# VectorE takes an output weight's low half first in a step; the opening norms two tiles at a time and evicts ahead of the last pair

## The chip, the cores and the metric

The kernel runs on one core of one Trainium2 chip. The metric is device time in microseconds (us) of one execution; several runs are given, and the figure is their median.

## The reference

One layer of a diffusion backbone is applied to 128 context tokens and to 2048 latent tokens, with the same weights but two modulations (`c_ctx` and `c`). Width 1024, everything in float32:

```
mod  = silu(c) @ w_mod + b_mod                      # shift, scale, gate, twice
h    = rmsnorm(x, norm1) * (1 + scale1) + shift1
z    = h @ w_in                                     # conv parts, q, k, v, o, gates
y_sc = short gated convolution of three 512-wide parts
h_m  = bidirectional mLSTM of q, k, v, gates; normed per head, times sigmoid(o)
x    = x + gate1 * (concat(y_sc, h_m) @ w_out)
h2   = rmsnorm(x, norm2) * (1 + scale2) + shift2
x    = x + gate2 * (silu(gg) * a @ w_down)          # a, gg: convolved halves of h2 @ w_up
y    = rmsnorm(x, final_norm)
```

Outputs are y for both token groups and the final mLSTM states of the context.

## The kernel before

All 2176 tokens are one sequence, held transposed: channels on the 128 partitions, tokens along the row. `BL` cuts it into six blocks: 0 to 4 of 384 tokens, 5 of 256. Block 0 holds the context tokens, so it has two spans with different modulation (`spans`). A 1024-wide activation is eight tiles, k = 0 to 7, of 128 channels.

Each float32 product is done as three matmuls of a narrower type: every operand is split in a high half (a rounded copy, made by ScalarE) and a low half (the rest, by a subtraction on VectorE or GpSimd), and `gemm` (L217) adds high x high, low x high and high x low for each k. So a tile is no use to TensorE until its low half is written: `hH`/`hL` for activations, `wh`/`wl` for weights.

**The opening** (L673 to L733). Its instructions keep the order in which they are written, engine by engine (`in_order(0)`, L733); those that are written later may be put between them by the planner, which orders each engine by its own estimate of when an operand is ready and by the order of writing. The modulation is computed on TensorE (`mods`), two column tiles at a time; in between come the norms. `apply` (L187) norms a block's tiles. For each k, VectorE multiplies (L196); for an even k ScalarE writes the high half (L200) and VectorE the low half (L201); for an odd k ScalarE adds the shift (L204), then copies the high half (L205), and GpSimd writes the low half (L206). `norm(b, rb, *ks)` (L696) calls it for the tiles that it names. Block 3 is normed in small pieces between the `mods`, block 4 at the end, four pairs of tiles.

`vg_first(k)` (L658) is block 3's value and gate product for one k: six accumulators, three chunks of 128 tokens by two column halves, each with three matmuls of 264 columns. Four of these are the four banks that `acc_tile` hands out in turn (`pa`, `pa1`); two are the halves of `y`, a two-bank tile. `vg_out` (L393) evicts one: GpSimd sets the ones column of a `row`, ScalarE copies (L396), SP's queue stores, and VectorE adds the gate bias from the same bank (L398). Then, at the end of the opening, `squares(5, ...)` (L172) sums the squares of block 5: ScalarE squares, VectorE adds (L184).

After that `vg((4,), hs, ws)` makes block 4's six value/gate tiles, with `prep(5, ss)` (L758) as a second generator that goes on by one step behind each tile. Its first step is empty, in its second `inv_rms` (L141) takes block 5's sum over the partitions on TensorE (L147) and its power on VectorE and GpSimd, in its third `apply` norms block 5. `vg((5,), ...)` and the heads (L426) follow, with side work in between: `mod_dve` computes the other 32 modulation tiles with products on VectorE, two per tile, into `y`; `first_stats` sums squares of blocks 0 to 2.

**The output projection.** From the mLSTM's last stage to the start of the feed-forward part each engine keeps the written order (`in_order(first)`, L1210). `out_proj` (L562) has 48 steps: one block and one 128-wide column tile of `w_out` each, one `gemm`. The head of a step on VectorE was written so (L597 to L610):

```
hook()                      # Feed: low halves of y for coming steps (L560)
load_r(k + 2)
while squared: add(...)     # token sums of squares (L589)
if len(behind) > 1: ...     # store, ScalarE's square
while trail: trail.pop()()  # wl of a weight split in the step before (L130)
```

`trail` has an entry only for the weights that `split_w` splits after step 20; GpSimd makes the low halves of the others. Then come the matmuls and VectorE's residual addition (L619), which frees the accumulator. From about step 22 on, `sums` (L249) puts work of the next stage behind each step: VectorE's product L272 and sums L283 to L291.

Of the kernel before, what the change touches and what calls it, by code (L numbers as in the profile page):

```python
# [10 lines left out]
F32 = mybir.dt.float32  # L11
F32R = mybir.dt.float32r
AF = mybir.ActivationFunctionType
# [7 lines left out]
KT = 8  # L21
# [30 lines left out]
def spans(t0, t1):  # L52

    return [(a, b, v) for a, b, v in ((t0, min(t1, P), 0), (max(t0, P), t1, 1)) if a < b]
# [3 lines left out]
def hymba_kernel(ctx: ExitStack, tc: tile.TileContext, I, O):  # L58
# [125 lines left out]
            V.tensor_add(ss[:, :n], ss[:, :n], sq[:, :n])  # L184
        return ss

    def apply(b, xt, norm, ks=range(KT), rb=None, pair=None):  # L187
        t0, n = BL[b]
        rb = spread(rcol(b), n) if rb is None else rb
        hH, hL = pair or h_pair()  # L190
        sh = 0 if norm == 0 else 24
        for k in ks:
            x = xt[k // 4][:, k % 4]
            for a, e, v in spans(t0, t0 + n):
                a, e = a - t0, e - t0
                V.scalar_tensor_tensor(x[:, a:e], x[:, a:e], ab[:, norm, k, v:v + 1], rb[:, a:e],  # L196
                                       op0=ALU.mult, op1=ALU.mult)
                sv = modT[:, sh + k, v:v + 1]
                if k % 2 == 0:
                    S.activation(hH[:, k, a:e], x[:, a:e], AF.Identity, bias=sv)  # L200
                    V.scalar_tensor_tensor(hL[:, k, a:e], x[:, a:e], sv, hH[:, k, a:e].bitcast(F32),  # L201
                                           op0=ALU.add, op1=ALU.subtract)
                else:
                    S.activation(x[:, a:e], x[:, a:e], AF.Identity, bias=sv)  # L204
                    S.activation(hH[:, k, a:e], x[:, a:e], AF.Copy)  # L205
                    G.tensor_sub(hL[:, k, a:e], x[:, a:e], hH[:, k, a:e].bitcast(F32))  # L206
        return hH, hL

    def h_pair():
# [158 lines left out]
    with ExitStack() as ph1:  # L368
# [193 lines left out]
        def out_proj(grps, defer, ws, hook):  # L562


            steps = [(g, m, b) for g, grp in enumerate(grps) for mp in range(0, KT, 2) for b in grp for m in (mp, mp + 1)]

            def load_r(k):
                if k < len(steps):
                    _, m, b = steps[k]
                    t0, n = BL[b]  # L570
                    xr = rp.tile([P, 384], F32, name="row")
                    Q.dma_start(xr[:, :n], I["x"][m][:, t0:t0 + n])
                    rows.append(xr)

            def close(b, m, xr):
                t0, n = BL[b]
                Q.dma_start(xD[m][:, t0:t0 + n], xr[:, :n])
                if m == 0:
                    second = b in grps[1]
                    sq = sss[b] = (rq if second else ssp).tile([P, 384], F32, name="cr" if second else "ss")  # L580
                else:
                    sq = sqp.tile([P, 384], F32, name="sq")
                S.activation(sq[:, :n], xr[:, :n], AF.Square)
                return b, m, sq

            def add(b, m, sq):
                n = BL[b][1]
                if m:
                    V.tensor_add(sss[b][:, :n], sss[b][:, :n], sq[:, :n])  # L589

            rows, got, trail, behind, squared, held, sss = [], [], [], [], [], [], {}
            for k in range(2):
                load_r(k)
            yield
            for k, (g, m, b) in enumerate(steps):
                grp, (t0, n) = grps[g], BL[b]
                hook()  # L597
                load_r(k + 2)
                while squared:
                    add(*squared.pop())  # L600
                if len(behind) > 1:
                    squared.append(close(*behind.pop(0)))
                while trail:
                    trail.pop()()
                if k - k % 4 + 4 < len(steps):
                    if k % 4 < (2 if k < 24 else 1):
                        got.extend(get_w(I["w_out"][steps[k + 4 + i][1]]) for i in range(1 if k < 24 else 2))
                    elif k % 4 > 1:
                        ws.append(split_w(got.pop(0), trail=trail if k > 20 else None))
                w, xr = ws[m % 2], rows.pop(0)  # L610
                acc = gemm(w, early[b], n)
                if k % 4 == 3:
                    del ws[:2]
                if held and k == held[0] + 4:
                    stats(held[1], [sss[b] for b in held[1]])
                    held = []
                for a, e, v in spans(t0, t0 + n):
                    a, e = a - t0, e - t0
                    V.scalar_tensor_tensor(xr[:, a:e], acc[:, a:e], modT[:, 16 + m, v:v + 1], xr[:, a:e],  # L619
                                           op0=ALU.mult, op1=ALU.add)  # L620
                behind.append((b, m, xr))
                if k % 16 == 15:
                    held = [k, grp]
                if k == len(steps) - 1:
                    for x in squared + [close(*x) for x in behind]:
                        add(*x)
                    defer.append(lambda: stats(grp, [sss[b] for b in grp]))
                hook(True)
                yield
# [3 lines left out]
        with tc.tile_pool(name="start", bufs=1, side="right") as stp:  # L633
# [24 lines left out]
            def vg_first(k):  # L658

                if k == 0:  # L660
                    y = pm.tile([P, 2, 512], F32, name="y")
                    vacc.extend([acc_tile() for _ in range(4)] + [y[:, 0], y[:, 1]])
                hH, hL = hs[3]
                for i in range(6):
                    j, c = divmod(i, 3)
                    w_h, w_l = (x[:, (k % 4) * 264:(k % 4 + 1) * 264] for x in ws[2 * j + k // 4])
                    a_h, a_l = hH[:, k, c * P:(c + 1) * P], hL[:, k, c * P:(c + 1) * P]
                    PE.matmul(vacc[i][:, :264], a_h, w_h, start=(k == 0), stop=False)
                    PE.matmul(vacc[i][:, :264], a_h, w_l, start=False, stop=False)
                    PE.matmul(vacc[i][:, :264], a_l, w_h, start=False, stop=(k == KT - 1))  # L670
# [23 lines left out]
            S.activation(rb, spread(rcol(3), 384)[:, :384], AF.Copy)  # L694

            def norm(b, rb, *ks):  # L696
                apply(b, xs[b], 0, ks, rb, hs[b])

            norm(3, rb, 0, 1)
            raw = get_vg(1)  # L700
# [24 lines left out]
            vg_first(5)  # L725
            norm(4, rb4, 4, 5)
            vg_first(6)
            norm(4, rb4, 6, 7)
            vg_first(7)
            ss = squares(5, xs[5])  # L730
            for i in range(6):
                vg_out(BL[3][0] // P + i % 3, i // 3, vacc[i])
            in_order(0)  # L733
            cB = stp.tile([P, 2, 1024], F32, name="cB")

# [20 lines left out]
                    yield  # L756

            def prep(b, ss):  # L758
                yield
                inv_rms(ss, BL[b][1], rcol(b))  # L760
                yield
                hs[b] = apply(b, xs[b], 0)
                yield
# [801 lines left out]
```

## Time and profile before

| | |
|---|---|
| median of 3 runs | 2499.62 us (2497.85 to 2501.0) |
| profiled execution | 2501.65 us |
| its span, first to last instruction | 2499.9 us |
| mean granted TensorE clock | 0.993 of full speed |
| busy: PE / weight loads / DVE / ACT / POOL | 98% / 94% / 66% / 45% / 21% |
| DMA | 447.61 MB, mean 179 GB/s |

PE is TensorE, PEld its weight loads, DVE is VectorE, ACT ScalarE, POOL GpSimd, SP SyncE with its DMA queue. Busy time is the time in which an engine has an instruction under way. An arrow `<-` names what ended an idle time, by the last semaphore event. The granted clock is TensorE's clock as a share of 2.4 GHz.

### The profile page before, as it was taken

To read this page: it belongs to the slowest core of one execution; us is meant where nothing else is said; L and a number is where in the kernel's file an instruction comes from. 1 tells how busy PE (TensorE), PEld (TensorE's weight loads), DVE (VectorE), ACT (ScalarE), POOL (GpSimd) and SP (SyncE) were. 2 spreads that over 40 slices of the span, in tenths; PEclk is the share of its full clock that TensorE was granted. 3 is DMA by queue.
4 is the path that set the end of the run, shared out by engine and by line. 5 is a ranking of instruction groups with operands and counts; after the bars stand their busy time and mean duration, and the time that the engine had idled before them with its cause. 6 is when DMAs were issued, how large, how long until landed. Compare 5 with 4: busy or idle time off the path is not lost. (4 is left out here: it accounts for less than half of the span.)

```text
span 2499.9 us, 42503 instructions
## 1 busy us (share of the span) xinstructions
PE 2450.5 (98%) x16127; PEld 2349.4 (94%) x16127; DVE 1638.6 (66%) x2682; ACT 1126.6 (45%) x2075; POOL 520.6 (21%) x468
## 2 busy tenths in 40 slices
PE   8899999999999999999999999999999999999998
PEld 8899999999999999989999999878888899999998
DVE  4893452332355675687668667877777786787586
ACT  3521243324445564465445445555555553444342
POOL 2433223211334351012112111122112200000000
PEclk9899999999999999999999999999999999999999
DMA  8673783265767886755126212622222286866674
GB/s 304 224 263 120 247 273 121 95 200 174 227 209 227 279 279 230 270 192 184 70 76 210 83 68 92 219 94 100 84 86 93 86 257 201 261 203 215 185 231 129
DMA packets 283102, 447.61 MB, mean 179 GB/s; under 512 B 23298, under 2 KB 208274, under 8 KB 280978
## 3 DMA queue, kind: packets, MB, share of 16 engines
q1 hardware_dynamic: 282898, 444.90, 54.1%
q8 instruction: 127, 2.08, 0.3%
q14 instruction: 77, 0.63, 0.1%
HBM read 336.82 MB, written 107.98 MB: 178 GB/s over the span
## 5 line engine op out<-in xcount | busy, mean ns | idle before, releaser
L224 PE MATMUL acc<-hH,wh 128*128 128x384 f32 (+1 forms) x1536 | 510.3, 332 | 1.0 <-ACT row L421 0.9
L226 PE MATMUL acc<-hH,wl 128*128 128x384 f32 (+1 forms) x1536 | 504.6, 329 | 2.9 <-DVE wl L130 2.6
L225 PE MATMUL acc<-hL,wh 128*128 128x384 f32 (+1 forms) x1536 | 503.1, 328 | 0.0
L1456 PE MATMUL d<-bh,wh 128*128 128x272 f32 x1232 | 356.4, 290 | 0.7 <-ACT raw L1314 0.7
L1458 PE MATMUL d<-bh,wl 128*128 128x272 f32 x1232 | 356.8, 290 | 0.0
L1457 PE MATMUL d<-bl,wh 128*128 128x272 f32 x1232 | 356.1, 289 | 0.0
L1302 PE MATMUL pa<-tH,wh 128*128 128x288 f32 (+1 forms) x1056 | 347.2, 329 | 3.2 <-DVE raw L1316 1.3
L1304 PE MATMUL pa<-tH,wl 128*128 128x288 f32 (+1 forms) x1056 | 345.9, 328 | 1.4 <-POOL wl L347 0.8
L1303 PE MATMUL pa<-tL,wh 128*128 128x288 f32 (+1 forms) x1056 | 346.5, 328 | 0.5 <-DVE tL L329 0.4
L347 POOL TENSOR_TENSOR wl<-st,wh 128x512 fp32r<-128x512 f32 x123 | 171.3, 1393 | 693.4 <-ACT wh L346 689.4
L226 PEld LDWEIGHTS acc<-hH,wl 128*128 128x128 f32 x1536 | 289.4, 188 | 5.7 <-DVE wl L130 5.4
L224 PEld LDWEIGHTS acc<-hH,wh 128*128 128x128 f32 x1536 | 289.7, 189 | 1.7 <-ACT row L421 1.3
L225 PEld LDWEIGHTS acc<-hL,wh 128*128 128x128 f32 x1536 | 289.7, 189 | 0.3 <-issue 0.2
L133 POOL TENSOR_TENSOR wl<-wst,wh 128x512 fp32r<-128x512 f32 (+1 forms) x136 | 198.7, 1484 | 424.4 <-ACT wh L127 371.1
L1245 DVE SCALAR_TENSOR_TENSOR tt<-raw,fw,tt 128x127 f32<-128x127 f32 (+4 forms) x264 | 245.6, 950 | 3.4 <-ACT tt L1251 2.3
L1456 PEld LDWEIGHTS d<-bh,wh 128*128 128x128 f32 x1232 | 232.6, 189 | 1.3 <-ACT raw L1314 1.1
L1457 PEld LDWEIGHTS d<-bl,wh 128*128 128x128 f32 x1232 | 232.6, 189 | 0.2
L1458 PEld LDWEIGHTS d<-bh,wl 128*128 128x128 f32 x1232 | 232.5, 189 | 0.0
L1302 PEld LDWEIGHTS pa<-tH,wh 128*128 128x128 f32 x1056 | 198.0, 188 | 19.7 <-ACT raw L1314 1.3
L1304 PEld LDWEIGHTS pa<-tH,wl 128*128 128x128 f32 x1056 | 198.6, 188 | 17.5 <-POOL wl L347 1.1
L1303 PEld LDWEIGHTS pa<-tL,wh 128*128 128x128 f32 x1056 | 198.2, 188 | 16.6 <-DVE tL L329 1.0
L346 ACT ACTIVATE wh<-s 128x512 fp32r<-128x512 f32 x176 | 110.7, 629 | 168.8 <-PE pc L1303 88.2
(268 smaller groups left out, 4830.9 us busy)
## 6 DMA issues: line engine op xcount, KB each, us to landing
st<-in_w_up SPq DMA_DIRECT2D x88, 512.0 KB, 4.6
us<-uD SPq DMA_DIRECT2D x48, 544.0 KB, 5.0
wst<-in_w_in SPq DMA_DIRECT2D x48, 512.0 KB, 3.9
uD<-tt SPq DMA_DIRECT2D x44, 544.0 KB, 2.7
R<-nD SPq DMA_DIRECT2D x34, 512.0 KB, 4.1
wm<-in_w_modr SPq DMA_DIRECT2D x32, 512.0 KB, 5.8
wst<-in_w_out SPq DMA_DIRECT2D x24, 512.0 KB, 3.7
st<-wsD SPq DMA_DIRECT2D x32, 384.0 KB, 3.9
```

The source lines that it names most:

```text
L133: G.tensor_sub(wl[:, a:a + n // 2], st[:, a:a + n // 2], wh[:, a:a + n // 2].bitcast(F32))
L224: PE.matmul(acc[:, :n], w_h, hH[:, k, :n], start=(k == 0), stop=False)
L225: PE.matmul(acc[:, :n], w_h, hL[:, k, :n], start=False, stop=False)
L226: PE.matmul(acc[:, :n], w_l, hH[:, k, :n], start=False, stop=(k == KT - 1))
L347: (G if on_pool else V).tensor_sub(wl, a, wh.bitcast(F32))
L1245: V.scalar_tensor_tensor(o, i, w, o, op0=ALU.mult, op1=ALU.add)
L1302: PE.matmul(acc, wh[:, w], rh, start=(kk == 0 and i in (0, 1, 5)), stop=False, skip_group_check=True)
L1303: PE.matmul(acc, wh[:, w], rl, start=False, stop=False, skip_group_check=True)
L1304: PE.matmul(acc, wl[:, w], rh, start=False, stop=(kk == 3), skip_group_check=True)
L1456: PE.matmul(acc, wh[:, c], uh, start=(kk == 0), stop=False)
L1457: PE.matmul(acc, wh[:, c], ul, start=False, stop=False)
L1458: PE.matmul(acc, wl[:, c], uh, start=False, stop=(kk == KH - 1))
```

## The change

Three edits. In `out_proj` the low half `wl` is taken at the head of a step, ahead of the feed and the token sums. `apply` takes groups of tiles: within a group first all products, then all ScalarE passes, then all low halves; `norm` passes its tiles as one group, every other caller keeps groups of one. In the opening `vg_first(7)` and three evictions stand ahead of the norm of block 4's last two tiles, the other three evictions behind it, and all ahead of block 5's squares; `prep` gets a second empty step.

```diff
-    def apply(b, xt, norm, ks=range(KT), rb=None, pair=None):
+    def apply(b, xt, norm, groups=[(k,) for k in range(KT)], rb=None, pair=None):
         t0, n = BL[b]
         rb = spread(rcol(b), n) if rb is None else rb
         hH, hL = pair or h_pair()
         sh = 0 if norm == 0 else 24
-        for k in ks:
-            x = xt[k // 4][:, k % 4]
-            for a, e, v in spans(t0, t0 + n):
-                a, e = a - t0, e - t0
-                V.scalar_tensor_tensor(x[:, a:e], x[:, a:e], ab[:, norm, k, v:v + 1], rb[:, a:e],
-                                       op0=ALU.mult, op1=ALU.mult)
-                sv = modT[:, sh + k, v:v + 1]
+        parts = [(a - t0, e - t0, v) for a, e, v in spans(t0, t0 + n)]
+        for ks in groups:
+            each = [(k, xt[k // 4][:, k % 4, a:e], hH[:, k, a:e], hL[:, k, a:e], modT[:, sh + k, v:v + 1], a, e, v)
+                    for k in ks for a, e, v in parts]
+            for k, x, h, l, sv, a, e, v in each:
+                V.scalar_tensor_tensor(x, x, ab[:, norm, k, v:v + 1], rb[:, a:e], op0=ALU.mult, op1=ALU.mult)
+            for k, x, h, l, sv, *_ in each:
                 if k % 2 == 0:
-                    S.activation(hH[:, k, a:e], x[:, a:e], AF.Identity, bias=sv)
-                    V.scalar_tensor_tensor(hL[:, k, a:e], x[:, a:e], sv, hH[:, k, a:e].bitcast(F32),
-                                           op0=ALU.add, op1=ALU.subtract)
+                    S.activation(h, x, AF.Identity, bias=sv)
                 else:
-                    S.activation(x[:, a:e], x[:, a:e], AF.Identity, bias=sv)
-                    S.activation(hH[:, k, a:e], x[:, a:e], AF.Copy)
-                    G.tensor_sub(hL[:, k, a:e], x[:, a:e], hH[:, k, a:e].bitcast(F32))
+                    S.activation(x, x, AF.Identity, bias=sv)
+                    S.activation(h, x, AF.Copy)
+            for k, x, h, l, sv, *_ in each:
+                if k % 2 == 0:
+                    V.scalar_tensor_tensor(l, x, sv, h.bitcast(F32), op0=ALU.add, op1=ALU.subtract)
+                else:
+                    G.tensor_sub(l, x, h.bitcast(F32))
         return hH, hL
...
             for k, (g, m, b) in enumerate(steps):
                 grp, (t0, n) = grps[g], BL[b]
+                while trail:
+                    trail.pop()()
                 hook()
                 load_r(k + 2)
                 while squared:
                     add(*squared.pop())
                 if len(behind) > 1:
                     squared.append(close(*behind.pop(0)))
-                while trail:
-                    trail.pop()()
...
             def norm(b, rb, *ks):
-                apply(b, xs[b], 0, ks, rb, hs[b])
+                apply(b, xs[b], 0, [ks], rb, hs[b])
...
             norm(4, rb4, 4, 5)
             vg_first(6)
+            vg_first(7)
+            for i in range(3):
+                vg_out(BL[3][0] // P + i, 0, vacc[i])
             norm(4, rb4, 6, 7)
-            vg_first(7)
+            for i in range(3):
+                vg_out(BL[3][0] // P + i, 1, vacc[3 + i])
             ss = squares(5, xs[5])
-            for i in range(6):
-                vg_out(BL[3][0] // P + i % 3, i // 3, vacc[i])
             in_order(0)
...
             def prep(b, ss):
+                yield
                 yield
                 inv_rms(ss, BL[b][1], rcol(b))
                 yield
```

## Rows read from the trace of the kernel before

**Rows 1.** The page: busy us, share of the span, instructions.
```profile
PE 2450.5 (98%) x16127; PEld 2349.4 (94%) x16127; DVE 1638.6 (66%) x2682; ACT 1126.6 (45%) x2075; POOL 520.6 (21%) x468
```

**Rows 2.** Stretches: length, PE, PEld, DVE, ACT, POOL busy, clock, DMA, GB/s.
```profile
62.00:75.00 13.00, 0.58 (x4) 0.43 (x3) 7.70 (x16) 8.98 (x22) 3.18 (x9) 0.63 0.51 206
...
82.00:100.00 18.00, 18.00 (x150) 18.00 (x150) 17.92 (x41) 11.63 (x29) 3.70 (x8) 1.00 0.69 223
```

**Rows 3.** TensorE's timeline, end of the opening: start, duration, line, idle before.
```profile
61.90 0.28 PE L670 MATMUL y<-wh,hL 128*128 128x264 f32 x1
74.61 0.99 PE L147 MATMUL st<-ones,ss 128*128 128x1 f32 x4 [12.42 <-DVE gates L398]
75.45 0.57 PE L411 MATMUL acc<-wh,hH 128*128 128x264 f32 x1
```

**Rows 4.** VectorE's timeline, norm of block 4 and squares of block 5.
```profile
64.04 0.95 DVE L201 SCALAR_TENSOR_TENSOR hL<-xs,modT,hH 128x384 fp32r<-128x384 f32 x1 [1.22 <-ACT hH L200]
64.91 1.12 DVE L196 SCALAR_TENSOR_TENSOR xs<-xs,ab,st 128x384 f32<-128x384 f32 x2
67.25 0.95 DVE L201 SCALAR_TENSOR_TENSOR hL<-xs,modT,hH 128x384 fp32r<-128x384 f32 x1 [1.22 <-ACT hH L200]
...
70.57 3.88 DVE L184 TENSOR_TENSOR ss<-ss,sq 128x256 f32<-128x256 f32 x7 [1.85 <-ACT sq L183]
```

**Rows 5.** ScalarE's timeline of the same stretch.
```profile
54.07 1.90 ACT L742 ACTIVATE cB<-cB 128x2048 f32<-128x2048 f32 x1
...
63.41 0.60 ACT L200 ACTIVATE hH<-xs,modT 128x384 fp32r<-128x384 f32 x1
65.55 0.61 ACT L204 ACTIVATE xs<-xs,modT 128x384 f32<-128x384 f32 x1 [1.54 <-DVE xs L196]
66.19 0.52 ACT L205 ACTIVATE hH<-xs 128x384 fp32r<-128x384 f32 x1
...
73.76 1.19 ACT L396 ACTIVATE row<-acc 128x256 f32<-128x256 f32 x4
```

**Rows 6.** Stretches of 2 us: length, PE busy, clock, DMA share, GB/s.
```profile
62.00:64.00 2.00, 0.18 (x2) 1.00 1.03 416
...
70.00:72.00 2.00, 0.00 (x0) 0.50 0.01 4
...
78.00:80.00 2.00, 2.00 (x16) 0.77 0.73 139
```

**Rows 7.** ScalarE's timeline: evictions of block 4's first, third and sixth tile.
```profile
80.25 0.39 ACT L396 ACTIVATE row<-acc 128x256 f32<-128x256 f32 x1 [0.65 <-PE acc L413]
...
86.28 0.37 ACT L396 ACTIVATE row<-acc 128x256 f32<-128x256 f32 x1
...
95.29 0.39 ACT L396 ACTIVATE row<-acc 128x256 f32<-128x256 f32 x1
```

**Rows 8.** TensorE's waits, 130 to 2500 us: total, times, longest.
```profile
PE acc L226 <- DVE wl L130: 2.6, 5, 0.7
```

**Rows 9.** GpSimd's timeline: low half of an odd tile of block 4.
```profile
63.58 1.00 POOL L206 TENSOR_TENSOR hL<-xs,hH 128x384 fp32r<-128x384 f32 x1 [2.22 <-ACT hH L205]
```

**Rows 10.** GpSimd's timeline: the last low half of block 5.
```profile
93.29 1.04 POOL L206 TENSOR_TENSOR hL<-xs,hH 128x256 fp32r<-128x256 f32 x1
```

**Rows 11.** VectorE's timeline: the head of a step of `out_proj`.
```profile
985.91 1.02 DVE L560 TENSOR_TENSOR hL<-xt,hH 128x384 fp32r<-128x384 f32 x2
986.85 0.55 DVE L589 TENSOR_TENSOR cr<-cr,sq 128x384 f32<-128x384 f32 x1
987.32 1.21 DVE L130 TENSOR_TENSOR wl<-wst,wh 128x1024 fp32r<-128x1024 f32 x1
```

**Rows 12.** TensorE's timeline: the matmul that waits for that `wl`.
```profile
988.59 0.44 PE L226 MATMUL acc<-hH,wl 128*128 128x384 f32 x1 [0.66 <-DVE wl L130]
```

**Rows 13.** ScalarE's timeline: the high half of the same weight.
```profile
981.86 1.06 ACT L127 ACTIVATE wh<-wst 128x1024 fp32r<-128x1024 f32 x1 [0.64 <-DMA wst<-in_w_out]
```

**Rows 14.** VectorE's timeline: a product of `mod_dve`.
```profile
77.34 1.23 DVE L751 SCALAR_TENSOR_TENSOR y<-wm,cB 128x1024 f32<-128x1024 f32 x1
```

## The prediction

> **What bounds the kernel now.** I read the busy times first: TensorE is busy 98% of the span [rows 1], so only what removes TensorE's idle time or raises its clock can move the end. The table by stretches says where the missing time is: in 62 to 75 us TensorE worked 0.58 us of 13.00, at a mean granted clock of 0.63; from 82 us it is full, and so is VectorE [rows 2]. TensorE's timeline gives the hole its edges: the last matmul of `vg_first(7)` starts at 61.90, and the next thing in its queue is `inv_rms` of block 5 at 74.61, after 12.42 us, put down to VectorE's gate additions [rows 3]. So behind the first value/gate tile lies a serial tail on VectorE and ScalarE: the norm of block 4, pair of tiles after pair, then block 5's squares and their adds, and only then the evictions of the six accumulators from 73.76 on [rows 4, 5]. The clock is 1.00 (2.4 GHz) in 62 to 64 us, 0.50 (1.2 GHz) by 70 us, and 0.77 on the mean in 78 to 80 us, when TensorE has worked again since 74.6 [rows 6]. So block 4's first tile, begun at 75.45 [rows 3], is evicted at 80.25, 4.8 us later, where three later tiles took 95.29 - 86.28 = 9.0 us, 3.0 each [rows 7]. The hole therefore costs 12.4 + (4.8 - 3.0) = 14.2 us.
>
> The table of waits has a smaller one late in the kernel: TensorE waits 2.6 us, in five pieces of at most 0.7, for the `wl` that VectorE writes in `out_proj` [rows 8].
>
> **The change part by part.**
>
> *Normed tiles two at a time.* Before, a pair of block 4 takes 67.25 - 64.04 = 3.21 us between two low-half subtractions [rows 4]. That is one chain: the subtraction of the even tile, VectorE's product of the odd tile, ScalarE's two passes of the odd tile, ScalarE's pass of the next even tile. In the new order both products come first, then ScalarE's three passes, then the subtractions. The chain is a product at 0.56 (half of 1.12), ScalarE's 0.60 and a subtraction at 0.95: 2.1 us [rows 4, 5]; ScalarE by itself needs 0.60 + 0.61 + 0.52 = 1.73, less [rows 5]. I take 2.0 per pair: the 0.95 holds a wait beside GpSimd's own subtraction of 1.00 us [rows 9], which in the new order lies mostly beside the products.
>
> On that point the Trainium skill, "SBUF — State Buffer", section "SBUF: two separate sides", is harsher than my 2.0: GpSimd and a VectorE operation with two SBUF inputs shut each other out for a whole instruction. The 0.95 us row fits it, as this subtraction began in the middle of GpSimd's. At its worst alignment the rule would hold the subtraction up for a whole GpSimd operation, a pair would take 2.8 us, and over the three pairs ahead of the first evictions the gain would be some 2 us smaller.
>
> *Evictions ahead of the last pair and of the squares.* At about 53.5 us ScalarE begins block 3's last two tiles (1.73), and there the planner has put the 1.90 us silu of `cB` [rows 5]; so it comes to block 4 at about 57.1. Three pairs at 2.0 end on it at 63.1; an eviction is 0.30 (1.19 for four [rows 5]) and VectorE's gate addition some 0.1 more, so the first bank is free at 63.5. TensorE idles 1.5 us instead of 12.4, and 62 to 64 us still shows clock 1.00 [rows 6]. The price: the additions wait for the evictions, and behind them in VectorE's queue stand the products of tiles 6 and 7, which start at 64.1. A product (0.56), ScalarE (1.73) and GpSimd (1.00) later, at 67.4, tile 7's low half is ready. Block 4's first value/gate tile comes to k = 7 at 63.5 + 7/8 x 3.0 = 66.1: another stall of 1.3 us. `inv_rms` of block 5, now between tiles, is still to be paid: 0.84 us at half clock (75.45 - 74.61 [rows 3]), about 0.5 at full. Sum: 14.2 - 1.5 - 1.3 - 0.5 = 10.9. I take 11.5, since the planner may fill the second stall with the next tile's first matmuls or put the silu elsewhere (up to 1.9). Bounds: with pairs as slow as before, 3.21, the three end 3.6 us later and the last adds 1.2, which leaves 6.1; with neither stall left it is 13.7.
>
> *One more empty step in `prep`.* It puts `inv_rms` and the norm of block 5 one tile of block 4 later, behind the third and the fourth. Block 5's squares with their seven adds (3.88 us [rows 4]) follow the last evictions, from about 67.3, so its sum is there by 72, before the third tile ends at 63.5 + 1.3 + 9.0 = 73.8. From the third tile's eviction to GpSimd's last low half it took 93.29 + 1.04 - 86.28 = 8.05 us before [rows 7, 10]. The fourth tile now ends at 77.3 (with the 0.5), so block 5 is ready at 85.4; TensorE comes to its first tile at 83.3 and to the last k at 85.9. No stall, but the margin falls from 95.29 + 2.6 - 94.33 = 3.6 us to 0.5.
>
> *VectorE takes `wl` first.* Only the weights split after step 20 go this way, twelve in all. From 985.91 on VectorE does two feed subtractions (1.02), a token add (0.47 to the next start), and then `wl`, from 987.32 to 988.53 [rows 11]; TensorE, which had waited 0.66 us, goes on at 988.59 [rows 12]. With `wl` at 985.91 it ends at 987.12, before TensorE's wait began at 987.93. A step without feed subtractions gains the 0.47 of the add alone. The rest keeps its place: the residual addition that frees the accumulator still comes behind all of these, no later; the feed subtractions come 1.21 us later, but for a step at least one ahead; the token sums have no reader until their group ends. What `wl` itself waits for, ScalarE's high half, is done at 981.86 + 1.06 = 982.92 [rows 13]. I take 2.3 of the 2.6; bounds 0 (VectorE has no idle time there, so that the next of its results may be late in place of each) and 2.6.
>
> *`apply` elsewhere* (blocks 0, 1, 2 and 5) has groups of one tile, and only block 0 with its two spans is reordered. I take 0, between -0.6 and 0.6 by one product.
>
> Sum: 11.5 + 2.3 = 13.8 us off the profiled execution's 2501.65: 2487.9. The median of the runs is 2.0 below that execution; against it 2485.8. I forecast 2486.
>
> **The rivals.**
>
> *A. The transfers don't come forward with TensorE* (12%). The DMA queues are full in 62 to 64 us (1.03) and idle in 70 to 72 (0.01) [rows 6]. If the heads' weights are limited by transfer, only that hole of about 6 us can be won back: 6 + 2.3 = 8.3 us, 2491. For it: the side work loads in the same stretch. Against: TensorE is full from 82 us on [rows 2], without a wait for a load.
>
> *B. The opening's hole stays* (8%), because `inv_rms` of block 5 is still put first on TensorE. Then the squares, now behind the evictions, hold TensorE until about 72 us with the clock down: 2 to 3 us won there, some 5 in all, 2495. For it: just that order stands in the old trace [rows 3]. Against: there the first tile could not have started either, as its bank's eviction began at 73.76; now the bank is free some 9 us ahead of the sum.
>
> *C. The other side: filler work on VectorE gets ahead of block 5* (5%). The `mod_dve` products (1.23 us each [rows 14]) need the accumulator pair that is now freed by 67.5, just when block 5's adds and norm come up, and VectorE is full later (17.92 of 18 us [rows 2]). Each product ahead of block 5's norm costs 1.23 us once the 0.5 us margin is gone. It decides from (13.8 + 0.5)/1.23 = 12 products on; with 16 the kernel loses 19.7 - 0.5 - 13.8 = 5.4 us: 2505.
>
> *D. The `wl` part gives nothing* (within the forecast's own range): 2488.
>
> **How the numbers follow.** The forecast with D, 2481 to 2490, has 70%; A 12%, B 8%, C 5%; 5% for stalls that come or go in the planned part behind the opening, either way. About 0.2% (5 us) is what can be told from no change, so faster is below 2494.6 and slower above 2504.6. Forecast, A and 3 of the rest: 0.85 faster. B and 1 of the rest: 0.09 same. C and 1 of the rest: 0.06 slower. The lower end: 13.7 + 2.6 = 16.3 off the median, 2483, less the 3 us by which the runs before differ: 2480. The upper end takes in A and the slow pairs (2499.6 - 6.1 = 2493.5): 2493.5.
>
> **What would show it.** Right: the stretch 62 to 75 us with over 9 us of TensorE work at clock 1.00; block 4's first tile ahead of `inv_rms` of block 5; a first eviction near 63 us, before the last pair; pairs near 2 us apart; no wait for `wl` in `out_proj`. Wrong: a wait at block 5's first tile (the margin is gone, or C), waits for weights in the heads (A), or in `out_proj` a wait for another result of VectorE, as long as the one for `wl` was.

## The result, and the profile after

The changed kernel takes 2486.8 us (median of 6 runs, 2485.47 to 2493.16) where the kernel before, run beside it, took 2499.91 (6 runs, 2497.01 to 2504.41). The ratio is 0.9944, 95% interval 0.9934 to 0.9955: 14.0 us less, by the interval 11.2 to 16.5. Timed once more on another occasion, beside the experiments, it gave 0.9944 again (0.9931 to 0.9956); a trace of that occasion is used below. The forecast was 2486.0 and a sum of 13.8 us. The profiled execution took 2485.78 us with a span of 2484.0; that of before took 2501.65, so between these two traces there are 15.9 us to be found.

The busy times on the page answer [rows 1]: TensorE has the same number of instructions in a shorter span, at the same share.

```profile
PE 2445.0 (98%) x16127; PEld 2344.0 (94%) x16127; DVE 1640.6 (66%) x2682; ACT 1124.8 (45%) x2075; POOL 526.3 (21%) x468
```

The first stretch of [rows 2], now: length, busy time of PE, PEld, DVE, ACT, POOL, granted clock, DMA share, GB/s.

```profile
62.00:75.00 13.00, 10.86 (x85) 10.44 (x86) 10.65 (x28) 9.31 (x24) 3.08 (x16) 1.00 0.90 299
```

In 62 to 75 us TensorE now works 10.86 us instead of 0.58, and the mean clock is 1.00 (2.4 GHz) instead of 0.63. TensorE's timeline gives the edges that [rows 3] gave: start, duration, line, and in brackets the idle time before.

```profile
61.38 0.28 PE L673 MATMUL y<-wh,hL 128*128 128x264 f32 x1
63.57 0.39 PE L414 MATMUL acc<-wh,hH 128*128 128x264 f32 x1 [1.91 <-DVE gates L401]
...
67.45 0.39 PE L416 MATMUL acc<-wh,hL 128*128 128x264 f32 x1 [0.57 <-POOL row L398]
...
75.43 0.50 PE L147 MATMUL st<-ones,ss 128*128 128x1 f32 x4
...
77.22 0.71 PE L158 MATMUL st<-ident,rc 128*128 128x128 f32 x4 [0.22 <-POOL rc L151]
```

The hole of 12.42 us is a wait of 1.91; block 4's first tile (L414) comes first, and the column sum of block 5's `inv_rms` (L147) and the spread of its result (L158, the start of `apply`) stand between later ones. ScalarE's timeline shows why the bank is free so early, and the evictions that answer [rows 7]:

```profile
55.14 1.90 ACT L747 ACTIVATE cB<-cB 128x2048 f32<-128x2048 f32 x1
...
62.95 0.91 ACT L399 ACTIVATE row<-acc 128x256 f32<-128x256 f32 x3
64.62 0.62 ACT L201 ACTIVATE hH<-xs,modT 128x384 fp32r<-128x384 f32 x1 [0.76 <-DVE xs L198]
...
68.30 0.37 ACT L399 ACTIVATE row<-acc 128x256 f32<-128x256 f32 x1
...
83.89 0.39 ACT L399 ACTIVATE row<-acc 128x256 f32<-128x256 f32 x1
```

Three accumulators are evicted from 62.95 on, before the last pair (64.62). Block 4's first tile leaves at 68.30 instead of 80.25, its sixth at 83.89 instead of 95.29: 11.40 us.

Where the 15.9 us of the two traces came from is read best from the start of the first matmul of each stage. The table has those starts in us, of the two kernels and of the experiments below, one execution each.

| kernel | heads | Sums | Mix | feed-forward | down |
|---|---|---|---|---|---|
| before | 106.69 | 499.68 | 662.02 | 1068.96 | 2004.33 |
| changed | 95.31 | 486.92 | 649.25 | 1052.99 | 1988.69 |
| changed, second occasion | 96.57 | 487.90 | 650.22 | 1054.22 | 1991.95 |
| e1_wl_only | 106.23 | 498.91 | 661.24 | 1065.22 | 2000.53 |
| e2_opening_only | 96.45 | 486.26 | 648.59 | 1055.34 | 1990.14 |
| e3_single_tiles | 100.93 | 490.39 | 652.70 | 1056.30 | 1991.34 |
| e3_timed | 102.50 | 492.22 | 654.55 | 1058.67 | 1993.60 |
| e4_late_evictions | 102.85 | 497.32 | 659.64 | 1063.63 | 1998.61 |
| e5_one_step | 97.71 | 490.70 | 653.01 | 1057.05 | 1991.72 |
| e6_three_yields | 97.35 | 487.24 | 649.55 | 1053.84 | 1990.00 |
| e7_silu_early | 94.64 | 485.83 | 648.15 | 1052.74 | 1990.28 |
| e8_products_first | 94.35 | 485.38 | 647.68 | 1051.58 | 1989.28 |
| e9_sum_before_filler | 93.09 | 486.18 | 648.48 | 1052.42 | 1987.64 |

The changed kernel leads by 11.4 us at the heads, 12.8 at the Sums and at the Mix, 16.0 at the feed-forward and 15.6 at the down projection. So the opening gives 11.4, the heads 1.4 more (the trace of before has there a wait of 0.9 us for a row, which is gone), and the stretch with `out_proj`, from Mix to feed-forward, 3.2. In its second trace the same kernel leads by 10.1, 11.8, 11.8, 14.7 (15 to 16 were expected there) and 12.4 us.

What lies between two executions of one program is mostly the granted clock, which falls to 0.50 (1.2 GHz) for a few microseconds in one and not in another. Stretches around two such places (length, PE, clock, DMA share, GB/s): the changed kernel, its second trace, and e6_three_yields.

```profile
380.00:490.00 110.00, 107.64 (x714) 0.98 0.29 95
1060.00:1076.00 16.00, 13.27 (x92) 1.00 0.72 244
```

```profile
1060.00:1076.00 16.00, 13.64 (x77) 0.79 0.64 217
```

```profile
380.00:490.00 110.00, 107.60 (x727) 1.00 0.29 94
```

From the heads to the Sums the four traces whose mean clock in 380 to 490 us is 1.00 (e2_opening_only, e3_single_tiles, e3_timed, e6_three_yields) take 389.5 to 389.9 us; the seven at 0.98 take 391.0 to 393.1, the two at 0.97 393.0 and 394.5. The down projection, from its first to its last matmul, follows the mean clock in 2200 to 2270 us: 480.3 to 480.8 us at 1.00, 482.1 to 483.6 at 0.98, 483.8 and 484.5 at 0.95. From feed-forward to down the changed kernel takes 935.7 us in its first trace and 937.7 in its second. So in each of these stages 2 to 4 us between two rows can belong to the execution and not to the kernel.

### The profile page after: what moved, and what is told of

Same layout as the page of the kernel before. It is cut to its first block, busy times and chain, and to the rows that moved or that the text cites. A ratio compares the mean times of both kernels' runs of the same rounds, so it can differ in the third digit from the quotient of the medians.

```text
span 2484.0 us, 42503 instructions
## 1 busy us (share of the span) xinstructions
PE 2445.0 (98%) x16127; PEld 2344.0 (94%) x16127; DVE 1640.6 (66%) x2682; ACT 1124.8 (45%) x2075; POOL 526.3 (21%) x468
```

## The experiments

**The two edits apart.** e1_wl_only is the kernel before with the `wl` edit alone; e2_opening_only is the changed kernel without it.

```diff
 # e1_wl_only, against the kernel before
+                while trail:
+                    trail.pop()()
                 hook()
 ...
-                while trail:
-                    trail.pop()()
```

> The kernel before with one edit: wl at the head of a step of out_proj; opening as before. My theory: nothing moves until the first wl (968.7 us before, 968.7 +- 1 here); from there to the first matmul of the feed-forward part (1069.0 before) 2.3 to 2.8 us are won, and TensorE's waits for wl fall from 2.6 us to about 0.5; timed 2.5 us faster (ratio 0.999). Rival D (VectorE is full there, the next of its results is late instead): the wl waits are replaced by others, the first feed-forward matmul stays within 0.5 us of 1069. A third, that the two parts help each other only together: under 1 us here.

> The changed kernel with the old place of wl in out_proj. My theory: the first heads matmul 11 to 11.5 us earlier than before (106.7), about 12.8 at the mLSTM's last stage (662.0 before), as in the changed kernel, and the wl waits of 2.6 us are back, so that the first feed-forward matmul comes 13 us earlier (1056) instead of 16; timed 12 to 13 us faster than before. Rival (what the opening wins is given back in the loading stages, and the difference is made later): under 8 us at 662.

Measured: e1_wl_only 0.9993 (0.9984 to 1.0001) of the kernel before, 1.7 us less, by the interval between 4.0 less and 0.2 more; e2_opening_only 0.9955 (0.9940 to 0.9970), 11.2 us less. Together 13.0, beside 14.0 for the whole: within the intervals the parts add. Timing alone can't settle a term of 2 or 3 us; the traces can. First TensorE's timeline of e1_wl_only, then the waits of its `out_proj` (total, times, longest), then those of e2_opening_only.

```profile
73.99 0.98 PE L147 MATMUL st<-ones,ss 128*128 128x1 f32 x4 [12.42 <-DVE gates L398]
```

```profile
PE acc L226 <- DVE wl L130: 0.9, 3, 0.4
```

```profile
PE acc L229 <- DVE wl L130: 2.4, 5, 0.7
```

The hole of 12.42 us stands untouched in e1_wl_only, and the waits for `wl` stand nearly untouched in e2_opening_only (2.6 before [rows 8]). The heads of e2_opening_only come 10.2 us before those of the old kernel, where 11 to 11.5 were expected. From the first Mix matmul to the first feed-forward matmul the two executions without the edit take 406.9 and 406.7 us; the eleven traces with it (two are of the changed kernel) take 403.6 to 404.6, mean 404.0, whatever their opening is like. That is 2.8 us for this edit.

**The evictions without the pairs.** e3_single_tiles norms one tile at a time, as before, with everything else of the change.

```diff
-                apply(b, xs[b], 0, [ks], rb, hs[b])
+                apply(b, xs[b], 0, [(k,) for k in ks], rb, hs[b])
```

> The changed kernel, but norm passes its tiles one at a time (groups of one), evictions and prep as changed. My theory: the evictions can only come when three pairs are normed, and a pair takes 3.2 us again in place of 1.8: first eviction near 66.5 us (62.95 changed), TensorE idle 5 us, last eviction of block 4's tiles 5 us later than in the changed kernel (83.89), so 6 to 7 us of the 11.4 remain; more is lost if the clock falls. Rival (the place of the evictions does it all, the pairs hide behind TensorE): within 1 us of the changed kernel.

The single run gave 2486.87 us, no worse than the changed kernel, though its heads began 5.6 us later and its feed-forward 3.3 later. Its down projection was some 2 us shorter than that of the changed kernel (480.7 us from the start of its first matmul to that of its last, against 482.7), at a clock of 1.00 in 2200 to 2270 us against 0.98; from heads to Sums it was 2.1 us shorter in the same way. One time with such a swing in it decides nothing, so the same kernel was timed.

> The kernel of e3_single_tiles again, timed in rounds, since in its one run a down-projection stage that was 2 us shorter than that of the changed kernel hid what the opening lost. By the traces it is 3.5 to 4.1 us behind at the Sums stage and 2.6 to 3.3 us at the feed-forward. Theory (pairs are worth it because the first eviction comes 2.9 us sooner): 2.5 to 4 us slower than the changed kernel, 2489 to 2490.5 us. Rival (the direct eviction alone gives the gain and the pairs nothing that lasts): within 1 us of the changed kernel, 2485.5 to 2487.5 us.

Ten runs gave 2492.6 (2487.2 to 2495.91), ratio 0.9971 (0.9962 to 0.9981): its interval lies wholly above that of the changed kernel, and the difference of the ratios is 0.0027, 6.7 us; by the two intervals, some 3 to 10. The rival is out, and the theory's 2.5 to 4 us lies at the low end of that. Here is the wait, and two stretches of 2 us of that trace (length, PE, PEld, DVE, ACT, POOL, clock, DMA, GB/s):

```profile
67.35 0.59 PE L414 MATMUL acc<-wh,hH 128*128 128x264 f32 x1 [5.06 <-DVE gates L401]
```

```profile
70.00:72.00 2.00, 2.00 (x11) 2.00 (x11) 0.38 (x3) 1.68 (x4) 0.53 (x1) 0.50 0.77 229
72.00:74.00 2.00, 2.00 (x18) 2.00 (x18) 0.13 (x1) 0.00 (x0) 0.67 (x7) 0.96 0.47 165
```

TensorE idles 5.06 us instead of 1.91, and the clock goes to 0.50 (1.2 GHz) until 72 us: 11 matmuls in 2 us instead of 18. The earlier execution of the same code had the same 5.06 us of idling, but its clock was already back at 1.00 in 70 to 72 us:

```profile
70.00:72.00 2.00, 2.00 (x19) 2.00 (x18) 0.34 (x2) 1.01 (x3) 1.20 (x7) 1.00 0.58 234
```

So what the hole costs beyond its length differs between executions of one program. That explains 0.6 of the 1.6 us between the two executions at the heads; 0.9 was there before the hole, as the mean clock in 10 to 22 us was 0.86 in e3_timed and 1.00 in e3_single_tiles.

**The pairs without the early evictions.** e4_late_evictions leaves the evictions and `vg_first(7)` in their old order.

```diff
-            vg_first(7)
-            for i in range(3):
-                vg_out(BL[3][0] // P + i, 0, vacc[i])
             norm(4, rb4, 6, 7)
-            for i in range(3):
-                vg_out(BL[3][0] // P + i, 1, vacc[3 + i])
+            vg_first(7)
             ss = squares(5, xs[5])
+            for i in range(6):
+                vg_out(BL[3][0] // P + i % 3, i // 3, vacc[i])
```

> The changed kernel, but the six evictions stand behind the norm and block 5's squares as before (vg_first(7) too); pairs and prep's second empty step as changed. My theory: TensorE takes inv_rms of block 5 first again and waits for the squares, which end near 70 us (norm 3.5 to 4 us earlier than before); idle 9 us, clock down again; 3 to 4 us of the 11.4 remain, less what prep's empty step costs at block 5's first tile (0 to 2 us). Rival (the pairs alone close the hole): 8 us or more remain.

One run, 2493.95 us. TensorE's timeline:

```profile
69.64 0.56 PE L147 MATMUL st<-ones,ss 128*128 128x1 f32 x2 [7.99 <-DVE gates L401]
```

`inv_rms` of block 5 is again the first thing in TensorE's queue, 7.99 us late (9 expected), and the heads come 3.8 us before those of the old kernel. At the heads the pairs alone are thus worth 3.8 us, the early evictions alone (e3_single_tiles and e3_timed) 5.8 and 4.2, both together 11.4, and 10.1 in the second trace of the changed kernel: more than the two added (8.0 to 9.6), by 0.5 to 3.4 us. Either alone leaves a hole of 5 to 8 us in which the clock falls, in all three traces, and behind the hole of e3_single_tiles TensorE waits another 1.7 us, in four pieces, for block 5's norm and tiles. With both, the wait is 1.91 us. The clock stayed at 1.00 behind it in the first trace, but not in the second, so the clock is only a part of the account. TensorE's timeline of the second trace, and a stretch of 2 us behind the wait (19 matmuls at 1.00 in the first trace):

```profile
63.55 0.45 PE L414 MATMUL acc<-wh,hH 128*128 128x264 f32 x1 [1.91 <-DVE gates L401]
```

```profile
64.00:66.00 2.00, 2.00 (x11) 2.00 (x11) 1.70 (x4) 1.38 (x3) 0.20 (x4) 0.50 0.85 314
```

**The empty step in `prep`.** e5_one_step takes the added step out, e6_three_yields puts in a third.

```diff
             def prep(b, ss):
                 yield
-                yield
                 inv_rms(ss, BL[b][1], rcol(b))
```

> The changed kernel with prep's second empty step taken out again. My prediction put the norm of block 5 one tile later by that step. Theory 1: without it TensorE takes inv_rms of block 5 one tile earlier, at about 71 us, and waits some 4 us for the sum, which was there at 75.2. Theory 2, since the planner goes by when the sum is ready: inv_rms and the norm stay where they are, within half a tile, and the stages agree with the changed kernel within 1 us.

> The changed kernel with a third empty step ahead of block 5's inverse norm in `prep`, the other way from e5_one_step; nothing is left out. Theory (the two empty steps put the norm's column sum behind 88 matmuls of block 4, and `apply` behind it; a step later the tiles of block 5 are made later than TensorE can use them): the column sum comes behind 96 matmuls, block 5's first tiles are late and TensorE waits 2 to 3.5 us for them after block 4's last tile; first heads matmul 2 to 3.5 us later than in the changed kernel. Rival (the steps move nothing that TensorE waits for, as with one step less): no such wait over 0.5 us, heads where the changed kernel has them.

e5_one_step took 2490.95 us in its one run; its opening is that of the changed kernel, 1.37 us later throughout (the mean clock in 10 to 22 us was 0.72, against 1.00), but for one wait. TensorE's timeline of it, and GpSimd's:

```profile
79.54 0.71 PE L158 MATMUL st<-ident,rc 128*128 128x128 f32 x4 [1.27 <-POOL rc L151]
```

```profile
78.74 0.10 POOL L398 MEMSET row<- 128x2 f32 x1 [2.64 <-DMA vD<-row]
78.79 0.70 POOL L151 TENSOR_TENSOR rc<-rc,mhalf 128x2 f32<-128x2 f32 x1
```

The column sum comes after the same 88 matmuls of block 4 with one empty step as with two: up to the second, the steps don't place it. All that the added one does is to put 8 matmuls rather than 7 between the column sum and the spread. That wait is 1.27 without it and 0.22 with it, but the step isn't shown to be the reason: with the step it is 1.08 in the second trace of the changed kernel and 0.88 in e2_opening_only. What sets it stands on GpSimd. Its `rc` comes behind a memset of a `row`, which the profile has waiting for a store: VectorE's part is done at 77.52 us in e5_one_step, and GpSimd begins at 78.79. The second trace of the changed kernel, TensorE and GpSimd:

```profile
78.50 0.71 PE L158 MATMUL st<-ident,rc 128*128 128x128 f32 x4 [1.08 <-POOL rc L151]
```

```profile
77.69 0.10 POOL L398 MEMSET row<- 128x2 f32 x1 [3.55 <-DMA vD<-row]
77.75 0.70 POOL L151 TENSOR_TENSOR rc<-rc,mhalf 128x2 f32<-128x2 f32 x1
```

VectorE is done at 76.55 us here, so GpSimd's `rc` begins 1.20 us late; in the first trace the memset came at 76.14, and `rc` began at 76.21, 0.08 after VectorE's part. A third step does what was expected: the column sum comes behind 96 matmuls, `apply` behind it, and block 5's first tile is late. TensorE's timeline of e6_three_yields:

```profile
84.77 0.39 PE L414 MATMUL acc<-wh,hH 128*128 128x264 f32 x1 [1.06 <-ACT hH L204]
```

Its heads come 2.0 us later than those of the changed kernel, the low end of the 2 to 3.5 expected (0.8 later than in its second trace). By the Sums 1.7 of that is gone (487.24 against 486.92), since its clock was 1.00 in 380 to 490 us, and its one time, 2485.37 us, shows nothing of it.

**What is left of the hole.** Three kernels take away, one after the other, what TensorE still waits for. e7_silu_early has the silu of `cB` (1.90 us, amid block 3's last pair in the changed kernel), and the loads that are issued with it, at a place where ScalarE is idle; e8_products_first has in addition VectorE's products of tiles 6 and 7 ahead of the first gate additions; e9_sum_before_filler in addition holds the first product of `mod_dve` until block 5's last addition.

```diff
+            late()
             norm(3, rb, 6, 7)
 ...
+            norm(4, rb4, 6, 7, part="products")
             for i in range(3):
                 vg_out(BL[3][0] // P + i, 0, vacc[i])
-            norm(4, rb4, 6, 7)
+            norm(4, rb4, 6, 7, part="rest")
 ...
+                        if mt == 16 and v == 0:
+                            tc.add_manual_dep(..., last_dve.name, ...)
```

> The changed kernel with the silu of cB (and the loads beside it) written ahead of the norm of block 3's last tiles, so that ScalarE does its 1.90 us in the idle 4.2 us before 53.0 and not in front of block 4's first pair. My theory (ScalarE's queue, not TensorE or VectorE, sets the first eviction): first eviction at 61.5 instead of 62.95, TensorE's first wait 0.4 to 0.6 us instead of 1.91, block 4's last tile evicted 1.4 us earlier (82.5); 1.4 us faster than the changed kernel, which is near what can be told. Rival (VectorE's queue or GpSimd sets it): first eviction within 0.4 us of 62.95.

> As e7, and VectorE's two products of block 4's last pair ahead of the first three gate additions (the evictions keep their place on ScalarE). My theory (the additions, waiting for ScalarE, hold the products up): tile 7's low half comes 0.6 to 0.8 us earlier than in e7 relative to the first eviction, TensorE's wait of 0.57 us for it goes; 0.5 us more than e7 by the trace, 2 us over the changed kernel. Rival (ScalarE's own three passes behind the evictions hold tile 7 up): the wait stays within 0.2 us of e7's.

> The kernel of e8_products_first with VectorE's first filler product of the modulation held until its last addition for block 5's sum of squares; nothing is left out. Theory: what is left of the hole in e8_products_first is the sum of block 5 coming late because filler products (1.23 us each) sit between its additions. Then TensorE's two waits there, 0.43 us for `ss` at the column sum and 1.14 us for `rc` at the spread, shrink to under 0.5 us together, the last eviction of block 4's tiles comes at 81.4 to 82.2 us (82.94 before it) and the time is about 1 us below e8_products_first, 2483 to 2484 us. Rival: the sum is set by ScalarE's squares and by the chain behind it on GpSimd, not by the filler; then the wait at the spread stays at 1 us or more and the time is that of e8_products_first.

ScalarE's timeline of e7_silu_early, then TensorE's:

```profile
48.91 1.90 ACT L729 ACTIVATE cB<-cB 128x2048 f32<-128x2048 f32 x1
...
61.50 0.91 ACT L399 ACTIVATE row<-acc 128x256 f32<-128x256 f32 x3
```

```profile
62.12 0.39 PE L414 MATMUL acc<-wh,hH 128*128 128x264 f32 x1 [0.28 <-DVE gates L401]
...
76.55 0.71 PE L158 MATMUL st<-ident,rc 128*128 128x128 f32 x4 [1.00 <-POOL rc L151]
```

The evictions begin at 61.50, 1.45 us sooner, and the first wait falls from 1.91 to 0.28. But the spread of block 5's `rc` is waited for 1.00 us, where the changed kernel has 0.22 in one trace and 1.08 in the other; the heads come 0.7 and 1.9 us sooner than in these. In e8_products_first the wait of 0.57 for tile 7 goes too (it is still there in e7_silu_early), but the first one is 0.62, a wait for block 5's sum (`ss`) is new, and at the spread there are 1.14, as its timeline of TensorE shows:

```profile
62.07 0.39 PE L416 MATMUL acc<-wh,hH 128*128 128x264 f32 x1 [0.62 <-DVE gates L403]
...
72.58 0.60 PE L147 MATMUL st<-ones,ss 128*128 128x1 f32 x4 [0.43 <-DVE ss L184]
...
76.27 0.71 PE L158 MATMUL st<-ident,rc 128*128 128x128 f32 x4 [1.14 <-POOL rc L151]
```

In e9_sum_before_filler the two waits for block 5's norm are gone, as expected: on VectorE's timeline the additions of block 5 stand in a row ahead of the first filler product, and the sum is there at 69.05 us. GpSimd's `rc` has moved ahead of the memset behind which it stood in e8_products_first, and begins 0.08 us after VectorE's, instead of 1.31.

```profile
66.47 2.58 DVE L184 TENSOR_TENSOR ss<-ss,sq 128x256 f32<-128x256 f32 x5
68.97 1.23 DVE L762 SCALAR_TENSOR_TENSOR y<-wm,cB 128x1024 f32<-128x1024 f32 x1
```

Its last matmul of block 4 starts at 80.45 us, against 82.55 in e8_products_first and 83.51 in the changed kernel. (ScalarE evicts that tile at 83.00 only, behind block 5's passes; so the expected 81.4 to 82.2 was missed, but TensorE waits for none of it.) The lead of 3.1 us over the changed kernel is 2.2 at the heads, since block 5's tiles, which TensorE reaches sooner, are not ready, and 0.7 at the Sums, because a wait for ScalarE's eviction of a row comes up in the heads that neither neighbour has. TensorE's timeline, and its waits from 97 to 485 us:

```profile
83.11 0.39 PE L418 MATMUL acc<-wh,hL 128*128 128x264 f32 x1 [0.30 <-POOL hL L211]
```

```profile
PE acc L229 <- ACT row L426: 1.6, 1, 1.6
```

The times: 0.9939 (0.9926 to 0.9953), 0.9934 (0.9921 to 0.9946) and 0.9938 (0.9926 to 0.9950) of the kernel before. e8_products_first has the lowest median of all, 2484.42 us, but none of the three can be told from the changed kernel's 0.9944. After the two big parts of the hole much of each further microsecond is met by the next wait.

## Why the prediction was right, point by point

*The hole and its price.* Right, with some luck in the size. TensorE's timeline has the start of block 5's first tile, before and changed:

```profile
95.05 0.28 PE L411 MATMUL acc<-wh,hH 128*128 128x264 f32 x1
```

```profile
83.63 0.28 PE L414 MATMUL acc<-wh,hH 128*128 128x264 f32 x1
```

Counted from the last matmul of `vg_first(7)` that is 95.05 - 61.90 = 33.15 and 83.63 - 61.38 = 22.25 us: 10.9 won, just what the terms gave, and not the 11.5 that was taken. The sixth eviction comes 11.40 us sooner because `vg_first(7)` also ended 0.5 sooner in this execution; the mean clock in 10 to 22 us was 0.86 in before and 1.00 in the changed kernel, and that stretch lies ahead of all that was changed. In the second trace of the changed kernel 9.6 us are won by the same count. The terms one by one: 1.91 of first wait (1.5 forecast); 1.2 at tile 7 (1.3); the column sum and the spread of block 5 make block 4's fourth tile 4.21 us long where the two before it take 2.90, 1.3 more, and 0.5 was forecast for the column sum alone.

*The first eviction.* Forecast 63.1, measured 62.95; pairs at 2.18 and 1.83 us, 2.0 taken. VectorE's timeline, for [rows 4], with the subtractions, a filler product and the last addition for block 5; and GpSimd's:

```profile
57.99 0.97 DVE L207 SCALAR_TENSOR_TENSOR hL<-xs,modT,hH 128x384 fp32r<-128x384 f32 x1 [1.83 <-ACT hH L201]
...
60.17 0.62 DVE L207 SCALAR_TENSOR_TENSOR hL<-xs,modT,hH 128x384 fp32r<-128x384 f32 x1 [0.16 <-ACT hH L201]
...
62.00 0.72 DVE L207 SCALAR_TENSOR_TENSOR hL<-xs,modT,hH 128x384 fp32r<-128x384 f32 x1 [0.16 <-ACT hH L201]
...
67.72 1.23 DVE L756 SCALAR_TENSOR_TENSOR y<-wm,cB 128x1024 f32<-128x1024 f32 x1
...
74.81 0.42 DVE L184 TENSOR_TENSOR ss<-ss,sq 128x256 f32<-128x256 f32 x1
```

```profile
57.53 1.02 POOL L209 TENSOR_TENSOR hL<-xt,hH 128x384 fp32r<-128x384 f32 x1 [3.37 <-ACT hH L204]
...
61.30 1.01 POOL L209 TENSOR_TENSOR hL<-xs,hH 128x384 fp32r<-128x384 f32 x1 [1.18 <-ACT hH L204]
...
66.40 1.00 POOL L209 TENSOR_TENSOR hL<-xs,hH 128x384 fp32r<-128x384 f32 x1 [2.17 <-ACT hH L204]
...
84.65 1.62 POOL L209 TENSOR_TENSOR hL<-xs,hH 128x256 fp32r<-128x256 f32 x1 [0.54 <-ACT hH L204]
```

*The stall at tile 7.* The low half is ready at 66.40 + 1.00 = 67.40 us, exactly as forecast, and releases the matmul at 67.45 (the wait is put down to the memset that stands next to it on GpSimd). The forecast stopped TensorE at the first matmul of k = 7, but only the last of a tile's 24 matmuls reads that low half; the two before it run at 66.37 and 66.60. So the idle time is 0.57, not 1.3. The tile as a whole takes 4.11 us to the start of the next, against 2.90 for that one, and so loses the 1.2 named above.

*Block 5's sum.* This step was out: forecast by 72 us, its last addition ends at 74.81 + 0.42 = 75.23. Products of `mod_dve` slip in between the additions (67.72 is the first), which is rival C's mechanism at four products instead of the twelve from which it would have decided. It costs at most 0.2 us here. In e8_products_first, where the rest has come forward, 0.43 us are a wait for the sum; the 1.14 at the spread come from the memset on GpSimd. In e9_sum_before_filler both are gone. The margin at block 5 went too: its last low half ends at 86.27 us and the matmul that reads it starts at 86.41, 0.1 us later, where 0.5 was forecast. From the fourth tile's eviction (77.09) to that low half it took 9.2 us instead of the 8.05 read in before, and GpSimd's last subtraction alone 1.62 instead of 1.04 [rows 10].

*The empty step.* No stall at block 5's first tile, as forecast, but not by the mechanism named: the column sum has its place with or without the step. That the step gains anything at the spread isn't shown.

*`wl` first.* 2.3 taken, 2.8 measured. On VectorE's timeline `wl` now stands ahead of the feed subtractions and the token add, where [rows 11] have it behind them:

```profile
973.11 1.22 DVE L130 TENSOR_TENSOR wl<-wst,wh 128x1024 fp32r<-128x1024 f32 x1
974.24 1.02 DVE L563 TENSOR_TENSOR hL<-xt,hH 128x384 fp32r<-128x384 f32 x2
975.18 0.55 DVE L592 TENSOR_TENSOR cr<-cr,sq 128x384 f32<-128x384 f32 x1
```

TensorE's waits name 2.1 us of the gain, as one wait of 0.5 remains where "no wait" was said; in these two traces the stretch from Mix to feed-forward is 3.2 us shorter, and the other 1.1 shows as busy time, with TensorE busy 403.05 us of it before and 401.98 now. (The matmul behind the wait in [rows 12] takes 0.44 us, where its neighbours take 0.34.)

```profile
PE acc L229 <- DVE wl L130: 0.5, 1, 0.5
```

*The rivals.* A (transfers): no wait for a load in the heads, and the whole lead of the opening arrives there. B: the order on TensorE is new, so no; e4_late_evictions is that rival's order brought about, and it costs 7.5 us at the heads. D: 2.8, not nothing. That the hole costs more than its length, by way of the clock, was in the sum (14.2 for a hole of 12.4); the rows bear it out, with 11 matmuls in 2 us at 0.50 where there are 18 or 19 at full clock.

*The sum.* Of the 15.9 us between the two traces 11.4 are the opening and 3.2 `out_proj`, both foreseen; the 1.4 in the heads were not. That the timing's 14.0 and the sum's 13.8 come so close is in part luck: the two terms missed by more, and two executions of the changed kernel alone lie 3.2 us apart in their spans (2484.0 and 2487.2).

*Still open.* From heads to Sums the clock and the waits for a row (0.9 in before, 1.3 in e1_wl_only, 1.4 in e4_late_evictions, 1.6 in e9_sum_before_filler) account for all traces to about 1 us; why that wait comes up in these four isn't known. Block 0's norm in its new order was taken at nothing, and no run takes it apart.

## What to carry to other kernels

When an engine idles behind a serial tail, ask first which instruction in its queue could start soonest and what keeps the bank that it needs; moving the evictions ahead of the tail's last part and shortening the tail gave 10.1 to 11.4 us together, though 3.8 and at most 5.8 apart. Once the hole is nearly closed, expect further gains to be met by the next wait, and look at what has slipped into the chain: filler products on VectorE, or a memset on GpSimd that waits for a buffer. Judge a term of a few microseconds by the stage's own start and end in several traces, and compare the granted clock there before a difference is laid to an edit: one time of e3_single_tiles hid 6 us, and one trace made an empty step look worth 1 us.

## What the runs showed of the hardware

A VectorE subtraction that meets GpSimd's ends 0.41 us after it each time: before, 64.04 + 0.95 = 64.99 after 63.58 + 1.00 = 64.58 [rows 4, 9]; now 57.99 + 0.97 = 58.96 after 57.53 + 1.02 = 58.55, and 62.00 + 0.72 = 62.72 after 61.30 + 1.01 = 62.31; without a meeting it takes 0.62 (60.17). In the new order the meetings cost 0.1 and 0.35 us. The trace agrees with the rule of the Trainium skill, "SBUF — State Buffer", section "SBUF: two separate sides", that the two shut each other out for a whole instruction; the worst alignment, from which the prediction worked out a loss of 2 us, did not come up.

The same wait of 1.91 us stands in five traces. The clock stayed at 1.00 behind it in four (the changed kernel, e2_opening_only, e5_one_step, e6_three_yields) and went to 0.50 in one, the second trace of the changed kernel. Waits of 5.06, 7.99 and 12.42 us took it to 0.50 in all five traces that have them, and for the same code and the same 5.06 us it was back at full speed by 70 us in one execution and only from 72 us in another. So the length of the short wait alone doesn't tell what the clock does behind it.
